# A macaron block on one core: the ScalarE half of each gate and up weight split is queued behind the last silu or copy into U given out before it

## The chip, the cores and the metric

The kernel runs on one core of one Trainium2 chip. The metric is the device time of one execution in microseconds (us), lower is better. Engine names are those of the profile: PE is TensorE's matmuls and PEld its weight loads, DVE is VectorE, ACT is ScalarE, POOL is GpSimd, SP is SyncE, which here issues the DMAs.

## The reference, cut to what matters

One layer: a half-step SwiGLU feed-forward block, a mixing layer with two kinds of attention, and a second feed-forward block. The change lies in the two feed-forward blocks, in their gate and up projections.

```
D_MODEL = 1024; SEQ = 1024; D_FF = 2816        # one layer, one batch

def _swiglu(x, w_gate, w_up, w_down):
    return (jax.nn.silu(x @ w_gate) * (x @ w_up)) @ w_down

f = _swiglu(_rmsnorm(x, ffn1_pre_g), ffn1_w_gate, ffn1_w_up, ffn1_w_down)
x = x + 0.5 * _rmsnorm(f, ffn1_post_g)
...
f = _swiglu(_rmsnorm(x, ffn2_pre_g), ffn2_w_gate, ffn2_w_up, ffn2_w_down)
x = x + 0.5 * _rmsnorm(f, ffn2_post_g)
```

## The kernel before

**Precision.** Every float32 operand is kept as two parts, a rounded "hi" and the rest "lo", and each product is made of three matmuls (hi hi, hi lo, lo hi; `PASSES`). Weights are split on the fly by `split`: ACT copies the raw tile into the hi half (L118), then POOL or DVE subtracts it from the raw tile to give the lo half (L119).

**Chunks and products.** A feed-forward block has 22 chunks of 128 hidden columns (`NF`). Chunk 0 is computed plainly; each of the chunks 1 to 21 is done as a Strassen-like block with seven products instead of eight. In chunks 1 to 20 PE runs them in the order P1, P6, P2, P7, P5, P4, P3 (`ORDER`; the last chunk has its own order), twelve matmuls of 128x512 each. They accumulate in four PSUM banks: P1 and P2 in `pa`, P6 in `pb`, P7 and P4 in `pc`, P5 and P3 in `pd`. Three of the weight tiles are raw; the others are sums and differences made on POOL (L218, L219 for P6; L228 for P3; L230 for P7).

**What follows a product** (`gate_up`). P1 is copied to a tile U2 on ACT (L425); P2 then adds onto P1 in the same bank, so PE can't begin P2 until that copy is done. P6 is added into U2 (L427), P7 into U3 (L430), P5 into U3 (L433), P4 into C21 (L439), P3 into U2 (L442), all on DVE, reading PSUM. When a quarter is complete (after P5, P2, P4, P3), `glu` does a silu on ACT (L462) and a multiplication on DVE (L463).

**Weights ahead.** The split weights lie in a pool of five buffers (`WBUFS`). `feed`, called ahead of each product, prepares the product four places further on; its buffer is that of the product just finished or running, so its split can't be written before that product is done with its weights.

**Extra steps.** After every odd chunk, `keep` queues the splits of the two hidden chunks just finished, for the down projection: copies on ACT (`high`, L348), subtractions (`low`, L351) and sums (`total`, L345) on DVE, and writes to DRAM (L352). They are handed out one step per product over the following two chunks, each step queued behind the last ACT and DVE instruction of that product (`tc.issue_after(self.mark[0])`, `tc.issue_after(self.mark[1])`). `self.mark[0]` is the last silu or copy into U2 that the program has given out.

**Order.** Each engine works its queue in order. Where the program leaves a choice, a scheduler fixes the order at build time; `tc.issue_after(ins)` adds an order (and no wait) behind `ins` for the instructions of its block on the engine of `ins`.

The chunk indices below count from 0 as in the code. A trailing ' marks products of the following chunk.

Of the kernel before, what the change touches and what calls it, by code (L numbers as in the profile page):

```python
# [36 lines left out]
def tile_macaron_block(ctx, tc, x, f1_pre, f1_post, f1_g, f1_u, f1_d, mix_pre, mix_post, w_qkv,  # L37
                       qg, kg, w_out, f2_pre, f2_post, f2_g, f2_u, f2_d, rope_a, rope_b, mask, out):
    nc = tc.nc
    PE, ACT, DVE, POOL, SP = nc.tensor, nc.scalar, nc.vector, nc.gpsimd, nc.sync  # L40
# [80 lines left out]
    class Ffn:  # L121
# [89 lines left out]
        def prepare(self, i, prod):  # L211
            a1, b1, a2, b2 = [self.RAW[i, d][:, :, :, 64 * b:64 * b + 64] for d in range(2) for b in range(2)]
            sub, add, tt = OP.subtract, OP.add, POOL.tensor_tensor
            if i + 1 < NF and prod in ("P1", "P4"):
                self.load_gu(i + 1, ("P1", "P4").index(prod))
            if prod == "P6":
                with tc.issue_after(self.order):
                    tt(b1, b1, b2, op=add)  # L218
                tt(a1, b1, a1, op=sub)  # L219
            if prod == "P7" and i == NF - 1:  # L220
                self.S["x"] = self.raw.tile([128, 2, 4, 128], F32, name="rawgu")[:, :, :, 0:64]
                tt(self.S["x"], b2, a1, op=sub)
            src = {"P1": a1, "P6": a1, "P7": self.S.get("x", a1), "P5": b1, "P2": a2, "P4": b2, "P3": a2}[prod]
            ins = self.split_w((i, prod), src, DVE if (i, prod) == (1, "P6") or prod in ("P5", "P3") else POOL)
            if prod == "P1":
                self.order = ins
            if prod == "P2":
                tt(a2, a2, a1, op=sub)  # L228
                if i < NF - 1:
                    tt(a1, b2, a1, op=sub)  # L230
# [992 lines left out]
```

## Time and profile before

| | before |
|---|---|
| median of 3 runs | 2129.7 us (2128.6 to 2131.04) |
| the profiled execution | 2127.34 us |
| its span, first to last instruction | 2125.4 us |
| PE busy | 2001.4 us (94%) |
| DVE / ACT / POOL busy | 1427.9 / 1033.2 / 863.0 us |
| mean granted TensorE clock | 0.984 |

The profile is of one execution. The span is 1.9 us shorter than that execution's time. A matmul counts as busy until its modelled end, so PE's 94% holds slow matmuls and pipeline refills too. Where an engine sat idle, the rows name the work whose end let it go on.

### The profile page before, as it was taken

What the parts mean: (1) busy time and instruction counts of PE and PEld (TensorE: products, weight loads), DVE (VectorE), ACT (ScalarE), POOL (GpSimd) and SP (SyncE); (2) the same over time, 40 slices, a digit from 0 to 9 for tenths busy, and PEclk for the clock granted to TensorE, in tenths of its full rate; (3) what the DMA queues carried; (4) which work ended last, traced back from release to release, by engine and by line L of the source; (5) the groups of instructions that cost most, each with busy time, mean ns of one, the idle gap of its engine ahead of it and who ended that gap; (6) DMA issues with size and microseconds to landing.
All of it is one profiled execution on the core that took longest, in us unless ns stands there. A gap on an engine that the chain in (4) does not pass through costs nothing.

```text
span 2125.4 us, 30587 instructions
## 1 busy us (share of the span) xinstructions
PE 2001.4 (94%) x10704; PEld 1686.3 (79%) x10704; DVE 1427.9 (67%) x2431; ACT 1033.2 (49%) x1977; POOL 863.0 (41%) x768
## 2 busy tenths in 40 slices
PE   7999999899899999999999999999999899999997
PEld 6777777777788899998999998877777677777886
DVE  7666666667556757766998886466666666666566
ACT  5533443434222644546999997234444443442223
POOL 4556555563000002024777887225656556520000
PEclk9999999999999999999999999999999999999999
DMA  4243333435975852232041552212333343369757
GB/s 139 71 138 126 132 139 112 146 121 205 337 268 195 309 154 93 74 104 63 1 134 55 168 142 84 95 60 98 121 129 138 119 139 129 129 237 327 249 196 278
DMA packets 234617, 316.39 MB, mean 149 GB/s; under 512 B 24672, under 2 KB 150624, under 8 KB 234336
## 3 DMA queue, kind: packets, MB, share of 16 engines
q1 hardware_dynamic: 234464, 314.44, 44.2%
q8 instruction: 85, 1.39, 0.3%
q14 instruction: 68, 0.56, 0.1%
HBM read 206.38 MB, written 108.00 MB: 148 GB/s over the span
## 4 chain that ended last, share of the span: by engine, by line
PE 56%; POOL 18%; ACT 8%; DVE 6%; issue 6%; DMA 4%; SPq 1%; POOLq 0%; DVEq 0%; ACTq 0%
PE pq L628 9%; POOL wgu L119 8%; PE pd L378 8%; PE pa L294 7%; PE pt L953 5%; PE pz L1091 4%; ACT wgu L118 3%; PE po L977 3%; PE sp L863 3%; PE pa L378 3%; POOL rawgu L219 3%; PE pb L378 3%; PE pc L378 3%; POOL rawgu L228 3%; POOL rawgu L218 3%
## 5 line engine op out<-in xcount | busy, mean ns | idle before, releaser
L119 POOL TENSOR_TENSOR wgu<-rawgu,wgu 128x512 fp32r<-128x512 f32 x216 | 308.7, 1438 | 433.3 <-ACT wgu L118 394.2
L118 ACT ACTIVATE wgu<-rawgu 128x512 fp32r<-128x512 f32 x302 | 184.8, 626 | 360.3 <-POOL rawgu L230 171.8
L294 PE MATMUL pa<-actT,wgu 128*128 128x512 f32 (+1 forms) x1080 | 288.4, 418 | 68.5 <-ACT U L425 67.6
L294 PEld LDWEIGHTS pa<-actT,wgu 128*128 128x128 f32 x1080 | 211.9, 203 | 132.7 <-ACT U L425 83.3
L378 PE MATMUL pd<-wgu,h 128*128 128x512 f32 x948 | 236.8, 394 | 10.2 <-DMA h<-hd 6.4
L118 ACT ACTIVATE wgu<-b 128x512 fp32r<-128x512 f32 x154 | 95.8, 630 | 269.6 <-PE pd L378 224.3
L378 PEld LDWEIGHTS pd<-wgu,h 128*128 128x128 f32 x948 | 179.3, 190 | 51.9 <-issue 6.7
L628 PE MATMUL pq<-wq,actT 128*128 128x256 f32 x1728 | 214.2, 281 | 0.7 <-DVE vst L639 0.7
L628 PEld LDWEIGHTS pq<-wq,actT 128*128 128x128 f32 x1728 | 206.0, 188 | 1.0 <-DVE vst L639 0.9
L119 DVE TENSOR_TENSOR wgu<-b,wgu 128x512 fp32r<-128x512 f32 x154 | 105.3, 689 | 112.3 <-ACT wgu L118 112.0
L73 POOL TENSOR_SCALAR gpost<-gpost 128x1024 f32<-128x1024 f32 x2 | 2.1, 1054 | 387.8 <-DMA gpost<-in_ffn_post_g_dram 387.8
L856 POOL TENSOR_SCALAR P<-P,il 128x1024 f32<-128x1024 f32 (+1 forms) x128 | 130.1, 1016 | 68.3 <-DVE il L855 65.5
L463 DVE TENSOR_TENSOR h<-h,C 64x512 f32<-64x512 f32 x42 | 49.6, 1182 | 146.8 <-ACT h L462 146.8
L957 DVE TENSOR_TENSOR PT<-pt,PT 128x512 fp32r<-128x512 f32 (+1 forms) x256 | 146.3, 613 | 2.3 <-ACT PT L956 2.2
L294 PE MATMUL pc<-actT,wgu 128*128 128x512 f32 x552 | 137.6, 398 | 4.8 <-DVE U L430 4.8
L294 PE MATMUL pd<-actT,wgu 128*128 128x512 f32 x552 | 136.1, 395 | 0.0
L956 ACT ACTIVATE PT<-pt 128x512 fp32r<-128x512 f32 (+1 forms) x256 | 125.0, 543 | 12.1 <-PE pt L953 8.3
L294 PEld LDWEIGHTS pc<-actT,wgu 128*128 128x128 f32 x552 | 102.2, 188 | 35.1 <-issue 11.1
L953 PE MATMUL pt<-identr,P 128*128 128x128 f32 x896 | 125.6, 275 | 3.1 <-ACT vst L791 2.4
L294 PEld LDWEIGHTS pd<-actT,wgu 128*128 128x128 f32 x552 | 103.5, 188 | 25.2
L294 PE MATMUL pb<-tx,wgu 128*128 128x512 f32 x504 | 122.9, 392 | 0.0
L294 PE MATMUL pc<-tx,wgu 128*128 128x512 f32 x504 | 122.5, 392 | 0.0
(205 smaller groups left out, 4075.3 us busy)
## 6 DMA issues: line engine op xcount, KB each, us to landing
hd<-y SPq DMA_DIRECT2D x154, 512.0 KB, 2.6
h<-hd SPq DMA_DIRECT2D x308, 256.0 KB, 4.0
rawgu<-in_ffn_w_gate_dram SPq DMA_DIRECT2D x88, 256.0 KB, 3.0
rawgu<-in_ffn_w_up_dram SPq DMA_DIRECT2D x88, 256.0 KB, 3.5
b<-in_ffn_w_down_dram SPq DMA_DIRECT2D x88, 256.0 KB, 5.1
bkT<-kd SPq DMA_DIRECT2D x32, 320.0 KB, 7.4
rawq<-in_w_qkv_dram SPq DMA_DIRECT2D x16, 512.0 KB, 5.0
bV<-vd SPq DMA_DIRECT2D x8, 640.0 KB, 4.2
```

The source lines that it names most:

```text
L118: ACT.activation(hi, raw, AF.Copy)
L119: return eng.tensor_tensor(lo, raw, f32(hi), op=OP.subtract).ins
L218: tt(b1, b1, b2, op=add)
L219: tt(a1, b1, a1, op=sub)
L294: PE.matmul(p[:, c0:c1, :], w[:, a, k, :], self.rhs(name, b, k)[:, c0:c1, :], start=(first and n == 0), stop=(n == 11), skip_group_check=True)
L378: PE.matmul(p, A[a][:, 128 * i:128 * i + 128], B[:, b, :], start=(first and start and j == js[0] and n == 0), stop=(end and j == js[-1] an ...
L628: PE.matmul(p, actT[:, a, k, T, :], WQ[j][:, b, k, :], start=(n == 0), stop=(n == 23))
L856: POOL.tensor_scalar(P[:, 0:w], P[:, 0:w], il, 1.0, op0=OP.mult, op1=OP.mult)
L953: PE.transpose(out=p[:, j, :], in_=col(P, b0 + j), identity=ident)
L956: ACT.activation(hv, p[:, 0:n, :], AF.Copy)
L957: DVE.tensor_tensor(lv, p[:, 0:n, :], f32(hv), op=OP.subtract)
L1091: PE.matmul(p[:, 512 * dh:512 * dh + 512], actT[:, a, c, T, :], WO[c][:, b, 512 * dh:512 * dh + 512], start=(n == 0), stop=(n == 23))
```

## The change

In `prepare`, the call of `split_w` is put into a block that queues its ACT instruction (the hi copy, L118) behind `self.mark[0]`, once there is one. The DVE or POOL half is not queued behind anything new, nor are the loads, the sums on POOL or the preparation for the down projection.

```diff
             src = {"P1": a1, "P6": a1, "P7": self.S.get("x", a1), "P5": b1, "P2": a2, "P4": b2, "P3": a2}[prod]
-            ins = self.split_w((i, prod), src, DVE if (i, prod) == (1, "P6") or prod in ("P5", "P3") else POOL)
+            with ExitStack() as behind:
+                if self.mark[0] is not None:
+                    behind.enter_context(tc.issue_after(self.mark[0]))
+                ins = self.split_w((i, prod), src, DVE if (i, prod) == (1, "P6") or prod in ("P5", "P3") else POOL)
             if prod == "P1":
                 self.order = ins
```

On ACT, the place where chunk 2 of the first block ends and chunk 3 begins. `wgu_950`, `971`, `995` and `1014` are the splits of chunk 3's P6, P2, P7 and P5; the three silus (L462, after the change L465) are those of chunk 2's P5, P4 and P3; `U2_1030<-pa_1017` is the copy of chunk 3's P1; `y_154` are copies of `keep`. Before:

```order
L118 ACTIVATE wgu_950<-rawgu_726 128x2x4x64
L118 ACTIVATE wgu_971<-rawgu_882 128x2x4x64
L462 ACTIVATE C21_880<-U3_943 64x512
L348 ACTIVATE y_154<-h_821 128x512
L118 ACTIVATE wgu_995<-rawgu_726 128x2x4x64
L462 ACTIVATE h_918<-C21_880 64x512
L118 ACTIVATE wgu_1014<-rawgu_726 128x2x4x64
L462 ACTIVATE C21_880<-U2_879 64x512
L348 ACTIVATE y_154<-h_590 128x512
L425 ACTIVATE U2_1030<-pa_1017 128x512
```

And with the change, the same place on ACT:

```order
L118 ACTIVATE wgu_950<-rawgu_726 128x2x4x64
L465 ACTIVATE C21_880<-U3_943 64x512
L351 ACTIVATE y_154<-h_821 128x512
L118 ACTIVATE wgu_971<-rawgu_882 128x2x4x64
L465 ACTIVATE h_918<-C21_880 64x512
L118 ACTIVATE wgu_995<-rawgu_726 128x2x4x64
L465 ACTIVATE C21_880<-U2_879 64x512
L351 ACTIVATE y_154<-h_590 128x512
L118 ACTIVATE wgu_1014<-rawgu_726 128x2x4x64
L428 ACTIVATE U2_1030<-pa_1017 128x512
```

Three splits have moved behind one silu each: P2's behind the silu of P5, P7's behind that of P4, P5's behind that of P3 (with the copies of `keep` that stand with these silus). The splits of P1, P6, P4 and P3 stand where they stood. The same holds in every chunk of both blocks.

On DVE, the same place: the row of chunk 3's P5 split (its lo half, `wgu_1014`) stood behind the addition of P3 into U2. Before:

```order
L439 TENSOR_TENSOR C21_880<-U2_879,pc_930 128x512
L463 TENSOR_TENSOR h_918<-h_918,C21_880 64x512
L351 TENSOR_TENSOR y_154<-h_821,y_154 128x512
L345 TENSOR_TENSOR h_993<-h_590,h_427 128x512
L442 TENSOR_TENSOR U2_879<-U2_879,pd_953 128x512
L119 TENSOR_TENSOR wgu_1014<-rawgu_726,wgu_1014 128x2x4x64
L463 TENSOR_TENSOR h_966<-C21_880,U2_879 64x512
L351 TENSOR_TENSOR y_154<-h_590,y_154 128x512
```

With the change it stands two rows further down, and nothing else on DVE has moved. POOL and PE have the same order as before; on SP one hidden-chunk write out of seven, every second chunk, stands ahead of two weight loads that it stood behind.

## Rows read from the trace of the kernel before

**Rows 1.** The page: the chain that ended last, shares by engine.
```profile
PE 56%; POOL 18%; ACT 8%; DVE 6%; issue 6%; DMA 4%; SPq 1%; POOLq 0%; DVEq 0%; ACTq 0%
```
**Rows 2.** Who waited for whom, whole run: us in total, times, longest us.
```profile
ACT wgu L118 <- POOL rawgu L230: 171.8, 40, 7.2
...
PE pa L294 <- ACT U L425: 67.6, 38, 2.5
```
**Rows 3.** Stretches: length, busy us (count) by engine, granted clock, DMA share, GB/s.
```profile
78.25:97.71 19.46, 19.46 (x86) 15.77 (x84) 11.83 (x14) 8.62 (x15) 10.75 (x8) 1.00 0.32 108
97.71:498.89 401.18, 366.99 (x1513) 289.64 (x1512) 255.00 (x296) 164.40 (x280) 231.54 (x163) 0.97 0.37 129
1471.10:1870.47 399.37, 364.95 (x1513) 288.35 (x1512) 254.95 (x296) 164.42 (x280) 231.21 (x163) 0.97 0.37 129
105.83:110.22 4.39, 4.39 (x12) 3.42 (x13) 2.41 (x4) 1.51 (x3) 1.46 (x1) 0.63 0.79 257
211.86:232.57 20.71, 19.69 (x86) 15.70 (x84) 12.61 (x15) 8.84 (x15) 12.06 (x10) 1.00 0.42 147
232.57:255.26 22.69, 19.93 (x86) 15.61 (x84) 15.83 (x18) 9.36 (x16) 13.62 (x10) 1.00 0.35 120
```
**Rows 4.** Timeline, chunk 2 into 3: start us, length us, instructions [idle before <- releaser].
```profile
91.71 1.78 DVE L345 TENSOR_TENSOR h<-h 128x512 f32<-128x512 f32 x1
92.97 1.15 ACT L118 ACTIVATE wgu<-rawgu 128x512 fp32r<-128x512 f32 x2 [4.39 <-POOL rawgu L219]
93.41 0.68 DVE L433 TENSOR_TENSOR U<-U,pd 128x512 f32<-128x512 f32 x1
93.68 3.01 POOL L119 TENSOR_TENSOR wgu<-rawgu,wgu 128x512 fp32r<-128x512 f32 x2 [0.74 <-ACT wgu L118]
94.18 0.63 ACT L462 ACTIVATE C<-U 64x512 f32<-64x512 f32 x1
...
95.64 0.69 DVE L439 TENSOR_TENSOR C<-U,pc 128x512 f32<-128x512 f32 x1
96.77 1.29 POOL L228 TENSOR_TENSOR rawgu<-rawgu 128x512 f32<-128x512 f32 x1
...
98.14 1.29 POOL L230 TENSOR_TENSOR rawgu<-rawgu 128x512 f32<-128x512 f32 x1
99.46 0.63 ACT L118 ACTIVATE wgu<-rawgu 128x512 fp32r<-128x512 f32 x1 [3.99 <-POOL rawgu L230]
100.12 0.63 ACT L462 ACTIVATE h<-C 64x512 f32<-64x512 f32 x1
...
100.78 1.23 DVE L463 TENSOR_TENSOR h<-h,C 64x512 f32<-64x512 f32 x1 [4.45 <-ACT h L462]
...
102.64 0.68 DVE L345 TENSOR_TENSOR h<-h 128x512 f32<-128x512 f32 x1
103.24 0.68 DVE L442 TENSOR_TENSOR U<-U,pd 128x512 f32<-128x512 f32 x1
...
104.01 0.63 ACT L462 ACTIVATE C<-U 64x512 f32<-64x512 f32 x1 [2.61 <-DVE U L442]
...
104.66 0.63 ACT L348 ACTIVATE y<-h 128x512 fp32r<-128x512 f32 x1
...
105.20 0.58 ACT L425 ACTIVATE U<-pa 128x512 f32<-128x512 f32 x1
...
105.83 4.59 PE L294 MATMUL pa<-actT,wgu 128*128 128x512 f32 x12 [2.40 <-ACT U L425]
```
**Rows 5.** Timeline, chunk 7 into 8, and P2 of chunk 9; same columns.
```profile
203.03 1.74 POOL L218 TENSOR_TENSOR rawgu<-rawgu 128x512 f32<-128x512 f32 x1
203.54 1.78 DVE L345 TENSOR_TENSOR y<-h 128x512 f32<-128x512 f32 x1
...
218.58 3.06 PE L294 MATMUL pa<-actT,wgu 128*128 128x512 f32 x12 [1.02 <-ACT U L425]
...
240.75 3.07 PE L294 MATMUL pa<-actT,wgu 128*128 128x512 f32 x12 [2.46 <-ACT U L425]
```

## The prediction

> **What bounds the kernel now.** I read the chain that ended last first: PE holds only 56% of it, and POOL holds 18% though its work is never the result of a stage [rows 1]. So in some stage PE waits for a chain that runs over POOL. The waits name the place: PE stood 67.6 us, 38 times, ahead of a matmul into `pa` until the copy into U (L425) was done, and ACT stood 171.8 us, 40 times, ahead of a split until POOL's L230 was done [rows 2]. Both are in the gate and up phase.
>
> The stretches size it. Chunk 2 of the first block runs without a stall in 19.46 us, with PE busy for all of them. That is PE's own time for a chunk. Chunks 3 to 20 take 401.18 us in the first block and 399.37 in the second, at a granted clock of 0.97 [rows 3]. Against 36 x 19.46 = 700.6 us that is 100.0 us too much, the most that this change could give. An even chunk is 20.71 long, 1.25 too much, and its P2 waited 1.02. An odd one is 22.69, 3.23 too much, and its P2 waited 2.46 [rows 3, 5]. The other 0.77 of the odd one are the refill of PE and smaller waits. The 18 even chunks make 22.5 us, so the 18 odd ones hold 77.5, or 4.3 each. What this has above 3.23 is clock: after the 2.40 us wait the granted clock was 0.63, so partly the lower level, 1.2 GHz, and P2 took 4.59 us instead of 3.07 [rows 3 to 5].
>
> The timeline from chunk 2 into 3 shows the chain [rows 4]. POOL ends L230 at 99.43. Then ACT does the hi half of P7's split (99.46), and only then the silu of P4 (100.12), although its input, the addition L439, was done at 96.33. The multiplication behind that silu (100.78) holds up DVE, so the addition of P3 into U2 comes at 103.24, the silu of P3 at 104.01, a copy of `keep` at 104.66, the copy of P1 at 105.20, and P2 on PE at 105.83, after 2.40 us of idleness. P2 could have begun at 103.43.
>
> **The change, part by part.** Nothing is added or removed, no instruction gets longer by itself, and PE and POOL keep their order. Three hi splits per chunk each go behind one silu.
>
> *P7's split behind the silu of P4* takes away the 3.8 us between that silu's input and its start. This is the gain.
>
> *P5's split behind the silu of P3* puts that silu 0.65 us (the step from 99.46 to 100.12) ahead of it, but the split still stands ahead of the copy of P1, so for the copy the sum is the same. PE needs P5's weights only after P2 and P7, some 5.6 us (two sevenths of 19.46) after P2 begins. Its lo half on DVE moves behind two instructions and frees a raw tile at most a microsecond later. The next weight loads are issued behind that and behind one hidden-chunk write on SP, which waits for a subtraction that is queued ahead of this lo half anyway. I cost both at nothing: the products P2 and P7 hide the split, and the POOL work of the current chunk hides the load. Were that cover gone, POOL's chain would move by what the load is late, at most that microsecond.
>
> *P2's split behind the silu of P5* costs something. That silu began at 94.18 because its addition (L433) ended at 94.09, so it doesn't come earlier. With it goes a copy of `keep` (0.65). P2's split then runs 95.49 to 96.12 instead of ending at 94.12, and its lo half on POOL starts at 96.19 instead of about 95.0. L228 follows at about 97.5 instead of 96.77.
>
> Now the sum for an odd chunk. The silu of P4 runs from 96.36, right behind P2's split. Three DVE instructions that read two SBUF tiles follow (the multiplication, a `low`, a `total`), at just the time in which POOL does the lo half, L228 and L230. Before, POOL had nothing to do then, but for the lo half of P7. Such meetings have prices in the rows: a multiplication 1.23 [rows 4], a `total` 1.78 against 0.68 without POOL [rows 4], a POOL sum 1.74 against 1.29 [rows 4, 5]. If all three meet a POOL instruction, they start at 97.0, 98.2 and 99.9, and the third ends at 101.6. The addition of P3 then runs to 102.28, the silu of P3 to 102.95, the copy of `keep` to 103.6, P5's split to 104.25, and the copy of P1 starts at 104.27 instead of 105.20. PE goes on 0.63 later, at 104.9, and has stood 1.47 us. P7's split, behind L230 at about 101.0, ends at 101.7 and is hidden behind DVE. If none meets, the three end by 99.0. P7's split then ends last, at 100.9, and the same steps behind it bring PE's wait to 0.1. These are the two ends; I take the upper one, since each of the three has a POOL instruction beside it.
>
> By the Trainium skill, SBUF — State Buffer, section Who interferes with whom, a DVE instruction with two SBUF inputs and a POOL instruction that reads SBUF hold one read port in turn, and the second is blocked for the whole of the first. By it all three would meet and the total is the one below; without it, it is the 2043 below. The 1.78 against 0.68 agrees with it; no row here shows which of the two goes first in the new order.
>
> For an even chunk the same steps hold with one `total` less and no copy of `keep` ahead of the copy of P1. These made it 2.46 - 1.02 = 1.44 better before [rows 5]. So 1.47 falls to about 0: no wait, and the 22.5 us come back.
>
> An odd chunk keeps 1.47 + 0.77 = 2.24 us. The clock should stay at the upper level: the even chunks, with waits of 1.0, show a granted clock of 1.00 [rows 3]. 18 x 2.24 = 40.3 stay, and 100.0 - 40.3 = 59.7 go. From the profiled 2127.3 that makes 2067.6. The median of before is 2.4 above the profiled execution, so I say 2069. Everything behind the phase starts as much earlier, and shows no bound that depends on the hour.
>
> **The rivals.**
> 1. *DVE and POOL miss each other.* An odd chunk keeps 0.1 + 0.77 = 0.87, so 84 us are gained: 2043. For it speaks that the 1.29 and 0.68 in the rows are as common as the long ones; against it, that both engines have a row of work at the same time.
> 2. *The meetings cost more*, or POOL gets behind them, and an odd chunk keeps all its 4.3 us with the low clock. Only the even chunks gain: 22.5 us, 2105. Against it: each of the three DVE instructions would have to lose about a third of a microsecond more than the longest in the rows.
> 3. *Slower.* P2's split waits for the silu of P5, and so POOL's whole run from the lo half of P2 to L230 hangs on DVE's addition of P5. That addition already stood behind a 1.78 us instruction [rows 4]. Each further meeting ahead of it moves the run, P7's split and the copy by 1.1. It decides when the copies come 59.7 / 36 = 1.7 us later than in the forecast. Two such meetings in every chunk, 2.2 us, give 36 x 2.2 - 59.7 = 19.5 us more than now: 2147. Against it: this part of DVE's order has not moved.
> 4. *The change does not reach the wait*, since something other than P7's split holds the silu of P4. Then 2127 to 2130. Against it: that silu starts 0.03 us behind the split.
>
> **How the numbers follow.** The forecast has 0.60, rival 1 0.20, rival 2 0.12, rival 3 0.04, rival 4 0.04. The forecast's own range is 2055 to 2085 (a wait of 0.8 to 2.4 in an odd chunk). With rival 1 it goes down to 2038; at the top I go to 2092, which takes in half of the way to rival 2. About 0.2 are left out. 0.2% (4 us) is about what a measurement of this kernel can tell from no change. Faster by more than that are the first three cases, 0.92; within it rival 4, 0.04; slower rival 3, 0.04.
>
> **What would show it.** In the changed trace: the silu of P4 directly behind P2's split and about 3 us ahead of P7's; PE's wait ahead of P2 gone in even chunks and about 1.5 us in odd ones, in all some 26 us instead of 67.6; chunks 3 to 20 in about 371 us; the granted clock there near 1.00; long DVE rows (1.2 to 1.8) beside L228 and L230. The prediction is wrong if even chunks still wait, if the low clock stays, or if the wait in odd chunks is far from 1.5.

## The result and the profile after

The changed kernel takes 2060.74 us (median of 4 runs, 2057.48 to 2062.22) against 2129.15 before: a ratio of 0.9676, 95% interval 0.9659 to 0.9693. That is 68 us less; 60 were forecast, and the time lies in the stated range. The profiled execution took 2062.22 us, its span is 2060.3. (One execution of a run further down, P7's move with both sums, took 6190 us; nothing explains it, and the ratio of that run leaves it out.)

The chain that ended last, and the waits of the whole run, answer to [rows 1, 2]:

```profile
PE 64%; DVE 16%; ACT 6%; DMA 5%; issue 5%; POOL 2%; SPq 1%; ACTq 0%; DVEq 0%; POOLq 0%
```

```profile
ACT wgu L118 <- POOL rawgu L233: 108.0, 40, 7.2
...
PE pa L297 <- ACT U L428: 23.8, 26, 2.2
```

POOL has left the chain (18% to 2%) and DVE has taken a part of it. PE's wait ahead of P2 has gone from 67.6 us to 23.8, of which 19.9 lie in the stretches below. (Line numbers have moved by three: L428 is the copy into U2, L445 the addition of P3, L465 the silu, L233 the sum for P7.)

The stretches, with the columns of [rows 3]: chunks 3 to 20 of each block, then chunks 7, 8, 9 and 10 of the first:

```profile
97.71:463.85 366.14, 354.77 (x1514) 282.53 (x1512) 280.25 (x297) 161.60 (x279) 234.64 (x163) 1.00 0.41 141
1439.01:1805.12 366.11, 353.98 (x1514) 282.15 (x1513) 278.02 (x297) 161.59 (x279) 233.61 (x163) 1.00 0.41 141
179.15:200.34 21.19, 19.96 (x86) 15.63 (x85) 17.62 (x18) 8.94 (x16) 14.50 (x10) 1.00 0.39 127
200.34:219.80 19.46, 19.46 (x85) 15.77 (x84) 13.77 (x16) 9.05 (x16) 11.50 (x10) 1.00 0.45 159
219.80:240.46 20.66, 19.72 (x85) 15.70 (x84) 16.09 (x18) 8.62 (x15) 12.95 (x10) 1.00 0.39 128
240.46:260.62 20.16, 19.73 (x86) 15.70 (x85) 14.13 (x17) 9.37 (x16) 12.33 (x10) 1.00 0.45 157
```

The 36 chunks take 732.3 us instead of 800.6, so 68.3 of the 100.0 are gone and 31.7 are left. The granted clock is 1.00, not 0.97. An even chunk can now run at PE's own 19.46.

The timeline from chunk 2 into 3, which answers to [rows 4]:

```profile
94.85 0.63 ACT L351 ACTIVATE y<-h 128x512 fp32r<-128x512 f32 x1
...
95.38 0.62 ACT L118 ACTIVATE wgu<-rawgu 128x512 fp32r<-128x512 f32 x1
95.65 0.69 DVE L442 TENSOR_TENSOR C<-U,pc 128x512 f32<-128x512 f32 x1
96.08 1.29 POOL L119 TENSOR_TENSOR wgu<-rawgu,wgu 128x512 fp32r<-128x512 f32 x1 [1.09 <-ACT wgu L118]
96.43 0.63 ACT L465 ACTIVATE h<-C 64x512 f32<-64x512 f32 x1 [0.43 <-DVE C L442]
97.09 0.83 DVE L466 TENSOR_TENSOR h<-h,C 64x512 f32<-64x512 f32 x1 [0.76 <-ACT h L465]
97.45 1.63 POOL L231 TENSOR_TENSOR rawgu<-rawgu 128x512 f32<-128x512 f32 x1
...
97.93 1.69 DVE L354 TENSOR_TENSOR y<-h,y 128x512 fp32r<-128x512 f32 x1
99.15 1.63 POOL L233 TENSOR_TENSOR rawgu<-rawgu 128x512 f32<-128x512 f32 x1
99.55 1.78 DVE L348 TENSOR_TENSOR h<-h 128x512 f32<-128x512 f32 x1
...
100.81 0.63 ACT L118 ACTIVATE wgu<-rawgu 128x512 fp32r<-128x512 f32 x1 [3.75 <-POOL rawgu L233]
101.25 0.68 DVE L445 TENSOR_TENSOR U<-U,pd 128x512 f32<-128x512 f32 x1
...
102.02 0.63 ACT L465 ACTIVATE C<-U 64x512 f32<-64x512 f32 x1 [0.57 <-DVE U L445]
...
103.21 0.61 ACT L118 ACTIVATE wgu<-rawgu 128x512 fp32r<-128x512 f32 x1
...
103.73 0.58 ACT L428 ACTIVATE U<-pa 128x512 f32<-128x512 f32 x1
...
104.36 1.90 PE L297 MATMUL pa<-actT,wgu 128*128 128x512 f32 x7 [0.93 <-ACT U L428]
```

The silu of P4 (96.43) is out of the queue behind P7's split and 3.7 us earlier. Now a subtraction (97.93) and a sum (99.55) of `keep`, each reading two SBUF tiles, meet POOL's two sums: 1.69 and 1.78 on DVE beside 1.63 and 1.63 on POOL. Alone they took about 0.7 and 1.29. ACT then stands 0.57 us with P7's split already done (101.44) until DVE's addition of P3, and PE waits 0.93.

### The profile page after: what moved, and what is told of

Same layout as the page of the kernel before. It is cut to its first block, busy times and chain, and to the rows that moved or that the text cites. A ratio compares the mean times of both kernels' runs of the same rounds, so it can differ in the third digit from the quotient of the medians.

```text
span 2060.3 us, 30607 instructions
## 1 busy us (share of the span) xinstructions
PE 1981.0 (96%) x10704; PEld 1676.3 (81%) x10704; DVE 1475.0 (72%) x2431; ACT 1030.5 (50%) x1977; POOL 866.7 (42%) x768
## 4 chain that ended last, share of the span: by engine, by line
PE 64%; DVE 16%; ACT 6%; DMA 5%; issue 5%; POOL 2%; SPq 1%; ACTq 0%; DVEq 0%; POOLq 0%
PE pq L631 9%; PE pd L381 8%; PE pa L297 7%; PE pc L297 6%; PE pt L956 5%; PE pz L1094 4%; DVE h L348 3%; DVE y L354 3%; PE po L980 3%; PE pa L381 3%; PE sp L866 3%; PE pb L381 3%; DVE h L466 3%; PE pc L381 3%; PE pb L297 2%
## 5 line engine op out<-in xcount | busy, mean ns | idle before, releaser
L119 POOL TENSOR_TENSOR wgu<-rawgu,wgu 128x512 fp32r<-128x512 f32 x216 | 302.6, 1402 | 362.5 <-ACT wgu L118 353.0
L118 ACT ACTIVATE wgu<-rawgu 128x512 fp32r<-128x512 f32 x302 | 187.8, 624 | 297.9 <-POOL rawgu L219 170.9
L297 PE MATMUL pa<-actT,wgu 128*128 128x512 f32 (+1 forms) x1080 | 268.0, 395 | 23.8 <-ACT U L428 23.8
L297 PEld LDWEIGHTS pa<-actT,wgu 128*128 128x128 f32 x1080 | 198.7, 189 | 78.8 <-ACT U L428 34.4
L118 ACT ACTIVATE wgu<-b 128x512 fp32r<-128x512 f32 x154 | 95.9, 630 | 269.8 <-PE pd L381 221.8
L354 DVE TENSOR_TENSOR y<-h,y 128x512 fp32r<-128x512 f32 x110 | 130.6, 1187 | 2.3
```

The lines of the kernel that those rows point to most:

```text
L118: ACT.activation(hi, raw, AF.Copy)
L119: return eng.tensor_tensor(lo, raw, f32(hi), op=OP.subtract).ins
L297: PE.matmul(p[:, c0:c1, :], w[:, a, k, :], self.rhs(name, b, k)[:, c0:c1, :], start=(first and n == 0), stop=(n == 11), skip_group_check=True)
L354: DVE.tensor_tensor(half(n, LO), S[k], f32(half(n, HI)), op=OP.subtract)
```

## The experiments

Three theories. Theory 1 is that of the prediction: the gain is the silu of P4, freed from P7's split; P2's move only costs; what is left in odd chunks is DVE meeting POOL. Theory 2: each of the three moves brings a share. Theory 3: what is left is POOL's run, through L230 (L233 after the change) and P7's split. All ratios are to runs of the kernel before beside them.

### One move at a time

The condition of the change gets a set of products, in each run another one:

```diff
-                if self.mark[0] is not None:
+                if self.mark[0] is not None and prod in ("P7",):
```

With `("P2",)` alone the scheduler puts P7's split behind the silu of P4 too, so that run is P2 with P7. No run moves P2's split alone.

P7 alone. 

> Only P7's split is queued behind the last silu; the splits of P2 and P5 stand as before the change. Theory 1 (the gain comes from the silu of P4, which no longer stands behind P7's split; P2's move only delays POOL): all of the gain and some more, since P2's lo half on POOL is not delayed by about a microsecond: no wait ahead of P2 in even chunks, 0 to 0.4 us in odd ones, 2040 to 2052 us. Theory 2 (each of the three moves brings a share): well above the changed kernel, 2075 to 2105.

P2 with P7. 

> P2's split is queued behind the last silu, which at build time also takes P7's split behind the silu of P4; P5's split stands ahead of the silu of P3 as before. Theory 1: the changed kernel's ACT stands idle for 0.57 us ahead of the silu of P3, so P5's split fits there and the copy of P1 comes about 0.6 us earlier: wait in odd chunks about 0.35 us, 2048 to 2054 us. Theory 2: P5's share of the gain is missing, 2075 to 2105.

P5 alone. 

> Only P5's split is queued behind the silu of P3; P7's split still stands ahead of the silu of P4. Theory 1: no gain, and the copy of P1 comes later by the 0.6 us of that split, which lay in an idle stretch of ACT before: waits of about 3.0 and 1.6 us, 2140 to 2155 us. Theory 2: a part of the gain, 2100 to 2115.

P7 with P5. 

> The splits of P7 and P5 are queued behind the silus, P2's is not. Theory 1: POOL's lo half of P2 follows that of P6 at once again, so L228 and L230 begin about a microsecond earlier than in the changed kernel; wait in odd chunks 0 to 0.5 us, 2040 to 2054 us. Theory 2: P2's share is missing, 2075 to 2090.

| splits behind a silu | us | ratio, 95% interval |
|---|---|---|
| P7 | 2038.9 | 0.9576 (0.9560 to 0.9592) |
| P7, P2 | 2051.9 | 0.9636 (0.9621 to 0.9650) |
| P7, P5 | 2051.3 | 0.9634 (0.9620 to 0.9648) |
| P7, P2, P5 (the change) | 2060.7 | 0.9676 (0.9659 to 0.9693) |
| P5 | 2154.3 | 1.0112 (1.0091 to 1.0132) |

Three fell into theory 1's ranges and P7 alone 1 us below its own; theory 2 is out, since P7's move alone gains 91 us, and each of the other two, added to it, takes back 12 to 13. P5's alone makes the kernel 24 us slower. In P7's run the lo half of P2 follows that of P6 on POOL at once, the silu of P3 comes 0.4 us earlier than in the changed kernel (3.92 us after the start of P1 at 96.91, against 4.31 after 97.71), P5's split fits into ACT's wait ahead of it, and P2 begins without a wait that the view shows:

```profile
92.90 3.01 POOL L119 TENSOR_TENSOR wgu<-rawgu,wgu 128x512 fp32r<-128x512 f32 x2 [0.74 <-ACT wgu L118]
...
99.02 1.15 ACT L118 ACTIVATE wgu<-rawgu 128x512 fp32r<-128x512 f32 x2 [2.75 <-POOL rawgu L233]
...
100.83 0.63 ACT L465 ACTIVATE C<-U 64x512 f32<-64x512 f32 x1 [0.66 <-DVE U L445]
...
102.02 0.58 ACT L428 ACTIVATE U<-pa 128x512 f32<-128x512 f32 x1
...
102.66 3.07 PE L297 MATMUL pa<-actT,wgu 128*128 128x512 f32 x12
```

With P5's move alone, the timeline of the same place shows the split pushed between the silu of P3 and the copy, while the long wait on ACT ahead of that silu, in which it lay before, stays empty; P2 then waits 2.95 us instead of 2.40:

```profile
103.95 0.63 ACT L465 ACTIVATE C<-U 64x512 f32<-64x512 f32 x1 [3.26 <-DVE U L445]
...
105.14 0.61 ACT L118 ACTIVATE wgu<-rawgu 128x512 fp32r<-128x512 f32 x1
105.66 0.58 ACT L428 ACTIVATE U<-pa 128x512 f32<-128x512 f32 x1
...
106.29 2.06 PE L297 MATMUL pa<-actT,wgu 128*128 128x512 f32 x4 [2.95 <-ACT U L428]
```

### What is left: DVE or POOL

The two `total` sums that stand ahead of additions on which PE waits are handed out one product later:

```diff
-                     [(high, 2, 4)], [(low, 2, 4), (total, 2, 5, 0)], [(high, 3, 5)], [(low, 3, 5), (total, 3, 4, 2)],
-                     [(high, 4, 2)], [(low, 4, 2), (total, 6, 1, 2)], [(high, 5, 3)], [(low, 5, 3), (high, 6, 6)],
+                     [(high, 2, 4)], [(low, 2, 4)], [(high, 3, 5), (total, 2, 5, 0)], [(low, 3, 5), (total, 3, 4, 2)],
+                     [(high, 4, 2)], [(low, 4, 2)], [(high, 5, 3), (total, 6, 1, 2)], [(low, 5, 3), (high, 6, 6)],
```

The first sum only, on the changed kernel. 

> The changed kernel, with one sum of keep (the second total, of the even chunks) handed out one product later, behind the addition of P3 into U2 instead of ahead of it. Theory 1 (the wait that is left in odd chunks is DVE's: three SBUF sums that meet POOL's work stand ahead of that addition): the silu of P3 comes up to 0.57 us earlier, until P7's split ahead of it on ACT holds it; wait in odd chunks 0.93 to about 0.4 us, 2048 to 2054 us. Theory 3 (the wait that is left is POOL's, through L230 and P7's split): no change, 2058 to 2062 us.

It took 2052.1 us, 0.9631 (0.9618 to 0.9644). The waits of odd chunks went from 0.93 to 0.39: DVE it was, for as much as that. What holds the silu of P3 now is P7's split, which waits for POOL, so theory 3 has the next 0.4:

```profile
100.72 0.63 ACT L118 ACTIVATE wgu<-rawgu 128x512 fp32r<-128x512 f32 x1 [3.76 <-POOL rawgu L233]
101.38 0.63 ACT L465 ACTIVATE C<-U 64x512 f32<-64x512 f32 x1
```

The waits ahead of P4 vanished too, but every even chunk now waited 0.4 to 0.8.

Both sums, on the changed kernel. 

> As the run before, and the other sum of this kind in the odd chunks, which stands ahead of the addition of P7 into U3, also one product later. Theory 1: PE's wait ahead of P4 (12 times 0.3 us) and the short waits ahead of P2 in even chunks (0.4 us) go as well, 2040 to 2048 us. Theory 3: 2054 to 2060 us.

This missed: 2058.0 us, 0.966 (0.9647 to 0.9673), worse than with one sum moved. Even chunks waited 0.7 to 1.1. The timeline, from P2 to P4 of chunk 5, shows something on POOL and on SP's queue that neither theory had:

```profile
145.11 0.38 SPq L183 DMA_DIRECT2D rawgu<-in_ffn_w_gate_dram  x1
...
146.78 0.32 SPq L355 DMA_DIRECT2D hd<-y  x1
...
147.15 1.12 SPq L183 DMA_DIRECT2D rawgu<-in_ffn_w_up_dram  x1
...
151.00 1.29 POOL L218 TENSOR_TENSOR rawgu<-rawgu 128x512 f32<-128x512 f32 x1 [1.07 <-DVE y L354]
151.11 1.72 DVE L348 TENSOR_TENSOR y<-h 128x512 f32<-128x512 f32 x1
...
152.36 1.62 POOL L219 TENSOR_TENSOR rawgu<-rawgu 128x512 f32<-128x512 f32 x1
```

POOL stood 1.07 us ahead of L218, the first sum that needs the next chunk's raw tile. The load of that tile's up half was issued 2 us after the gate half, since a write to DRAM had come between them on SP and waited for a DVE subtraction. The row names DVE; but the load issued at 147.15 took 3.7 us to land, so it was there at about 150.9, just ahead of L218.

All of this was there with the first sum moved alone:

```profile
147.14 0.42 SPq L183 DMA_DIRECT2D rawgu<-in_ffn_w_up_dram  x1
...
150.36 0.68 DVE L348 TENSOR_TENSOR y<-h 128x512 f32<-128x512 f32 x1
...
151.06 1.30 POOL L218 TENSOR_TENSOR rawgu<-rawgu 128x512 f32<-128x512 f32 x1 [1.17 <-DVE y L348]
...
152.43 1.30 POOL L219 TENSOR_TENSOR rawgu<-rawgu 128x512 f32<-128x512 f32 x1
```

So the late load can explain why even chunks wait in both runs, but not why the second sum made it worse. That sum (150.36 here) had already ended when the late L218 began, so P4 had no wait left that its move could take away. Moved behind the addition of P7, it meets L219: 1.72 us instead of 0.68 on DVE, 1.62 instead of 1.30 on POOL. PE's waits ahead of P2 went from 20.5 us to 25.2 in the two profiled executions, which is about what the medians differ by (5.9 us); no run tests this part by itself.

To test the place of the load, the subtraction goes one product later too:

```diff
-[(low, 3, 5), (total, 3, 4, 2)],
-                     [(high, 4, 2)],
+[(total, 3, 4, 2)],
+                     [(low, 3, 5), (high, 4, 2)],
```

> The run with all three moves and both sums later (2058 us), and one subtraction of keep (the fourth low, in odd chunks) also one product later, so that its write to DRAM stands behind the two loads of the next raw weight tile on SP, not between them. In that run the second load was issued 2 us behind the first and landed just as POOL's L218 began, after POOL had been idle for 1.1 us. Theory 4 (that load's place on SP is why the run missed its 2040 to 2048): the load comes about 1.6 us earlier, POOL's wait goes, the waits ahead of P2 in even chunks fall from 0.8 to 0 to 0.3 us, 2038 to 2048 us. If the place of the load does not matter: 2054 to 2060 us.

It took 2047.7 us, 0.9617 (0.9601 to 0.9633). The load comes at 145.18, the wait ahead of L218 is gone, and even chunks wait 0.15:

```profile
144.74 0.38 SPq L183 DMA_DIRECT2D rawgu<-in_ffn_w_gate_dram  x1
145.18 0.50 SPq L183 DMA_DIRECT2D rawgu<-in_ffn_w_up_dram  x1
...
147.61 0.34 SPq L355 DMA_DIRECT2D hd<-y  x1
...
148.94 1.15 DVE L354 TENSOR_TENSOR y<-h,y 128x512 fp32r<-128x512 f32 x1
...
149.55 1.69 POOL L218 TENSOR_TENSOR rawgu<-rawgu 128x512 f32<-128x512 f32 x1
```

L218 begins here before the subtraction that the row had named (L354) is done, so that was not what it waited for. So the load's place on SP cost 10 us and was the cause of the miss: without it the time lies at the upper end of the range for both sums.

### P7's move with the sums later

P7 alone and both sums. 

> Only P7's split queued behind the last silu, and both sums one product later. Theory 1: what the run with P7's split alone had left (0.8 us in every second chunk) goes as well, 14 us less than that run: 2024 to 2032 us. Theory 3: the same as that run, 2036 to 2040 us.

2028.4 us, 0.9517 (0.9504 to 0.9530), the best version. Of the gate and up phase nothing is left to gain here: the first block's 18 chunks in 350.40 us are 19.47 each, with PE busy throughout, and the second block's take 349.20.

```profile
96.97:447.37 350.40, 350.40 (x1513) 283.97 (x1512) 279.95 (x298) 163.13 (x280) 239.40 (x163) 1.00 0.42 147
```

P2 and P7 and both sums. 

> The splits of P2 and P7 queued behind the silus, P5's as before the change, both sums one product later. It stands beside the run with P7's split alone and the same sums (2028 us) and shows what P2's move costs by itself when DVE is out of the way. Theory 1 (P2's move delays POOL by about a microsecond, which then reaches the copy through P7's split): a wait of up to 0.5 us in odd chunks, 2030 to 2042 us. Theory 3 (POOL's run was the limit all along in the kernel with all three moves): 2048 to 2058 us.

2043.5 us, 0.9595 (0.9581 to 0.9609), a little above theory 1's range. It is 15 us more than without P2's move, with DVE out of the way: odd chunks wait 0.4 again, which makes some 11.6 us of it (20.11 instead of 19.47 in each). P7's split, for which POOL's L233 must be done, begins 3.10 us after P1 (99.07), and 2.11 in the run without P2's move (96.97). Here, then there:

```profile
102.17 1.16 ACT L118 ACTIVATE wgu<-rawgu 128x512 fp32r<-128x512 f32 x2 [3.75 <-POOL rawgu L233]
```

```profile
99.08 1.16 ACT L118 ACTIVATE wgu<-rawgu 128x512 fp32r<-128x512 f32 x2 [2.76 <-POOL rawgu L233]
```

P2's move costs by itself, through POOL's run, and the odd chunk of the changed kernel has two limits one behind the other, DVE at 0.93 and POOL at 0.4.

## Why the prediction was right, point by point

- **Where the time lay: right.** The 100.0 us between the chunks and PE's own 19.46 were nearly all that could be had: in the best version the 36 chunks run at 19.47 and 19.40 each, 101 us less than before, and the whole took 2028.4 beside 2130.05 for the kernel before, 102 us less.
- **P7's split behind the silu of P4 is the gain: right, and shown.** By itself it gains 91 us. The silu was forecast for 96.36 and came at 96.43.
- **P2's split behind the silu of P5 costs: right, and shown.** Its lo half was forecast for 96.19 and came at 96.08, with POOL idle for 1.09 us ahead of it; undone, 9 us come back (2060.7 to 2051.3).
- **P5's split costs nothing: wrong.** I set its 0.65 us as equal ahead of the silu and behind it. But ACT stands and waits ahead of that silu (0.57 us in the changed kernel, 2.61 before), so ahead of it the split is free and behind it it lies on the path. Undone, 9 us come back (2060.7 to 2051.9); moved alone, it costs 24. The forecast of the time was not hurt by this, since its sum follows the new order on ACT step by step with the split in it; wrong is that leaving the split where it stood would have been no better.
- **DVE meets POOL: right, one price too high.** All three instructions met POOL's work, as I had chosen. The subtraction and the sum took 1.69 and 1.78, but the multiplication 0.83, where I had put 1.23 from a row of before (100.78). There the POOL instruction beside it ended 0.69 us after the multiplication had begun (row below), here 0.28 us after it (96.08 + 1.29 against 97.09). Of the copy's 0.54 us ahead of the forecast (103.73 against 104.27) this is 0.4. So the wait was 0.93, not 1.47, and this is the term of the sum that was mis-sized. It overrates what is left by 18 x 0.54 = 10 us; 31.7 were left instead of 40.3. (A slip besides: 2067.6 and 2.4 make 2070, not 2069.)

```profile
100.17 1.30 POOL L119 TENSOR_TENSOR wgu<-rawgu,wgu 128x512 fp32r<-128x512 f32 x1 [0.74 <-ACT wgu L118]
```

- **Even chunks wait no more: right in 12 of 18.** The other six wait about 0.4. They stand behind the odd chunks in which P4 did not wait (chunks 9 and 10 above, against 7 and 8). In just these six the up half of the next raw tile took 4.8 to 5.8 us to land, against 3.7 to 4.5 in the other twelve, and L218 began 0.5 to 1.1 us later in its chunk. In five of them POOL stood idle until the load was there. Chunk 7, then chunk 9:

```profile
191.50 1.74 POOL L218 TENSOR_TENSOR rawgu<-rawgu 128x512 f32<-128x512 f32 x1
...
227.29 0.67 SPq L183 DMA_DIRECT2D rawgu<-in_ffn_w_up_dram  x1
...
233.22 1.29 POOL L218 TENSOR_TENSOR rawgu<-rawgu 128x512 f32<-128x512 f32 x1 [1.03 <-DMA rawgu<-in_ffn_w_up_dram]
```

- **P5's later weight load costs nothing: nearly right in the sum, wrong in the mechanism.** The POOL work of the chunk was to hide it, and in these chunks it does not. In chunk 9 the load is issued 7.49 us after P1 begins; with P2 and P7 moved and P5's split left in its place, 6.16 us (225.71 after 219.55), and there, as with P7 alone, no even chunk waits. No run moves the load by itself. It costs little, since the sum on DVE then misses the late L218 and P4 does not wait: such a pair of chunks takes 40.82 us against 40.65, about 1 us for all six. With the sums moved, a late load cost 10 us.
- **The clock: right.** The longest wait ahead of P2 in the two stretches is 1.2 us, against 2.5 before, and 1.00 was granted in both.
- The span shrank by 65.1 us, the stretches by 68.3. The other 3 us lie between the two blocks (972.21 us before, 975.16 after) and were not followed up; executions of the changed kernel differ by up to 4.7 us, and by the medians the gain is 68.4.

## What to carry to other kernels

On an engine that works in order, look at what each waiting instruction has behind it: a short instruction whose input is ready, queued behind one that waits for a slow engine, costs the whole wait, and one swap may be worth more than all of a blanket rule (91 us against 68 here). Then look at the reverse for each instruction that the same rule moves: in front of a wait it was free, behind it it is on the path. And when work is moved to an earlier time, ask which engine is busy then, and what follows it on the queue that issues the loads.

## What was not expected

- The blanket order is worse than its best part: 2060.7 us for the three moves, 2038.9 for one of them, 2154.3 for another.
- Moving a sum out of a collision moved a load: a DVE subtraction that ended later held a DRAM write on SP, and that a weight load behind it, which cost 10 us (2058.0 against 2047.7). The second sum, moved as well, only met POOL's next instruction and made the kernel slower (2052.1 to 2058.0).
- A wait's named releaser can be another: ahead of L218 the view named a DVE instruction, and moving the DMA's place took the wait away, with that instruction still running.
